# RWKV, attention and expert trunk on one core: `w_out` products leave the last RWKV steps, output norms go to VectorE with the bonus made ahead, two experts' matrices issued together

## The chip, the core and the metric

One core of a Trainium2 chip runs the kernel. A core has a matmul engine (TensorE, PE in the rows), VectorE (DVE), ScalarE (ACT), GpSimd (POOL) and SyncE (SP, which here only issues transfers), each with an instruction stream of its own; they meet through semaphores. Sixteen DMA engines carry the transfers that SP, ACT and POOL issue. The metric is the device time of one execution in microseconds, as the median of several runs.

## What is computed

Two layers of a trunk over 512 latent tokens and 256 context tokens, 1024 channels, float32. In each layer three mixers read slices of one input projection: a two-directional RWKV recurrence (256 channels, four heads), an S5 recurrence (256) and windowed attention (512). Their outputs side by side go through `w_out`, a residual and a norm; then each token goes through two of 32 experts.

```python
def trunk_layer(x, xc, ...):                # last layer: no context output
    proj = (x * (1.0 + sc1) + sh1) @ w_in   # and the same of xc
    yr, yr_c = rwkv_mixer(...); ys, ys_c = s5_mixer(...); ya, ya_c = attention_mixer(...)
    mix = jnp.concatenate([yr, ys, ya], axis=-1) @ w_out
    x = layer_norm(DEEPNORM_ALPHA * x + gt1 * mix, ln1_g, ln1_b)
    h = x * (1.0 + sc2) + sh2
    y = hier_moe(h, *moe_params)            # top 2 of 8 experts in the best of 4 groups
    x = layer_norm(DEEPNORM_ALPHA * x + gt2 * y, ln2_g, ln2_b)

def rwkv_output(y, feats, g2, r_k, gn_w, gn_b):
    mu = jnp.mean(y, axis=-1, keepdims=True)
    var = jnp.mean(jnp.square(y - mu), axis=-1, keepdims=True)
    yn = ((y - mu) * lax.rsqrt(var + GN_EPS)).reshape(B, L, RWKV_WIDTH) * gn_w + gn_b
    bonus = jnp.sum(r * k_sum * r_k, axis=-1, keepdims=True) * v
    gate = jax.nn.sigmoid(g_lo) @ g2
    return (yn + bonus) * gate
```

## The kernel before

Tokens go in tiles of 128: layer 0 has six (0 and 1 are context, 2 to 5 latent), layer 1 only the four latent ones. A layer runs through these stages:

- **Input side**: the projection and S5.
- **RWKV** (`rwkv`): `front` and `back` build each tile's features; `inverse` and `solves` prepare chunks; then twelve `steps`, n = 0 to 11, carry the state through the chunks in both directions at once. The directions use banks of the matmul's accumulators named f and g. Within a step L631 multiplies by the state, L633 adds on DVE, L640 forms the new state, L647 and L653 put it away on DVE; L672 and L676 are the step's output, and L682 adds it to the tile's `y`. When all steps are through, `finish` takes tiles 3 and 4, then 2 and 5: mean, variance (the squares `sq` are made on POOL, L699), the reciprocal root on POOL (L702, L703), a multiply on DVE (L706), `gn_w`, `gn_b` on POOL (L707, L708), the bonus `v` times `bon` on DVE (L710), added on POOL (L711), the gate from a matmul (L713) multiplied on DVE (L714). The result is turned on PE (L59) and copied by ACT to `yo`. The context tiles finish after step 3.
- **Mixing** (`mixing`), a generator that other work draws from. `part(i)` multiplies the S5 and attention rows of tile i by `w_out`: twelve products of 128x512 on PE (L1602), then DVE gates them and adds the residual (L1609, L1610, two of each), and ACT stores the sum to memory. `norm(i)` loads it back as `q` (L1635, ACT), adds the RWKV rows' four products (L1644) to it (L1650), takes moments (L1651, L1652), makes `h` (L1655, L1656) and its transposes; `logits` is the router's matmul (L1394, L1397, L1400). `affine` makes the residual of the next norm from `q` (L1668, L1669). `choose` picks groups and experts for two tiles with some fifty small DVE instructions and scatters tokens to a table (L1472, POOL); `Route.finish` reads the table back (L1502, L1504, L1506, L1509) and makes the index lists.
- **Experts**: POOL gathers tokens (L1869) and 32 experts run in turn. `Weights.get(e)` issues three matrices of 2 MB each on SP; three experts have buffers.

What sets the order: the program order is the priority, and a scheduler then orders each engine's stream by it and by the data. The table `FILL` says, for each point of `rwkv`, how many units of attention, of the modulation and of `mixing` are drawn in there. After steps 6, 8 and 9 it drew the six parts, after 10 and 11 the norms of tiles 0 and 1 and their choice. `k.rest` and `k.normed` tell the caller how far the generator is to be run behind `rwkv` and behind the first expert's weights. `q` and two small tiles of the norms had three buffers.

Of the kernel before, what the change touches and what calls it, by code (L numbers as in the profile page):

```python
# [1545 lines left out]
def mixing(k, l, sO, sR, before, yd, ys, x_src, x1, hd, NTOK):  # L1546
# [132 lines left out]
    late = {}  # L1679
    if t0 == 0:  # L1680
        for j in range(2):
            hT, late[j] = norm(j)
# [4 lines left out]
        rank = rt.choose([0, 1])
        k.rest = True
        yield
    for j, i in enumerate((3, 4)):  # L1690
        hT, late[i] = norm(i)
        if j == 0 and t0 == 0:
            rank()
        rt.logits(j, hT)
        yield
    late[3]()
    hT, late[2] = norm(2)
    rank = rt.choose([3 - t0, 4 - t0])
    rt.logits(0, hT)
    late[4]()  # L1700
    hT, late[5] = norm(5)
    rt.logits(1, hT)
# [581 lines left out]
```

## Time and profile before

| | us |
|---|---|
| median of three runs (2838.5 to 2843.27) | 2841.53 |
| the profiled execution, its own time | 2848.87 |
| its span in the trace | 2847.1 |
| layer 0: last steps, finish, norms, router (740 to 910) | 170 |
| layer 1: the same (2160 to 2277) | 117 |
| layer 0: the first expert's matmul starts at | 910.08 |
| layer 1: the same | 2276.55 |

The span is the profiled execution without what lies around it; times in the rows count from its start. A row of a timeline gives the start, the length, the engine, the line, the operation with its output and inputs and, in brackets, how long the engine stood idle before it and what ended that. PE rows put several instructions together (x32), and one product of the kernel appears there as two records. In the stage table each engine has its busy time and, in brackets, its instructions; PEclk is TensorE's granted clock as a share of its upper level.

### The profile page before, as it was taken

The numbers are of one execution on the slowest core, as the hardware profiler recorded it, in microseconds if no ns is written. First come the engines' busy times: TensorE is split into PE (matmuls) and PEld (weight loads), VectorE is DVE, ScalarE is ACT, GpSimd is POOL, SyncE is SP. The second block draws the span as 40 slices with busy tenths as digits, with TensorE's granted clock in tenths as the row PEclk, the third lists the DMA queues.
The fourth block names the chain that finished last, engine by engine and source line by source line (L and its number), as shares of the span: only waits on it lengthen the run. The fifth ranks groups of instructions, "written<-read, shape, count | busy, mean of one in ns | idle before, by whom it ended". The sixth has DMA issues, their size and how long they took to land. (4 is left out here: it accounts for less than half of the span.)

```text
span 2847.1 us, 43425 instructions
## 1 busy us (share of the span) xinstructions
PE 2222.6 (78%) x16189; PEld 1485.8 (52%) x16189; DVE 1165.4 (41%) x2836; ACT 517.5 (18%) x1264; POOL 805.1 (28%) x1160
## 2 busy tenths in 40 slices
PE   5898677888973978999856788787797397888882
PEld 3787455666542544555525676565554254454441
DVE  7972556563384000101026873656545611111113
ACT  3222333222010000101015122333120100000001
POOL 2651534330152111101016653434334210111002
PEclk8999788598986999999987898688798698999996
DMA  8334567665547899989974325556774799989994
GB/s 243 95 95 118 152 189 200 173 183 172 191 172 239 347 416 368 392 336 375 380 280 117 82 57 148 134 143 162 217 226 155 229 378 417 419 348 367 376 421 185
DMA packets 413931, 690.01 MB, mean 242 GB/s; under 512 B 148882, under 2 KB 318610, under 8 KB 397232
## 3 DMA queue, kind: packets, MB, share of 16 engines
q1 hardware_dynamic: 310368, 594.85, 58.7%
q10 hardware_dynamic: 74960, 56.54, 6.8%
q0 software_dynamic: 28288, 34.32, 3.7%
q8 instruction: 210, 3.44, 0.5%
q14 instruction: 105, 0.86, 0.1%
HBM read 606.46 MB, written 95.47 MB: 247 GB/s over the span
## 5 line engine op out<-in xcount | busy, mean ns | idle before, releaser
L1776 PE MATMUL b_m<-w,xT 128*64 128x256 f32 x4928 | 596.2, 398 | 128.4 <-DMA w<-in_expert_w_gate_dram 80.4
L1776 PEld LDWEIGHTS b_m<-w,xT 128*64 128x64 f32 x4928 | 391.8, 143 | 335.2 <-issue 148.1
L243 PE MATMUL b_m<-xT,win 128*128 128x256 f32 (+1 forms) x1416 | 275.9, 355 | 8.5 <-POOL xT L167 3.7
L243 PEld LDWEIGHTS b_m<-xT,win 128*128 128x128 f32 x1416 | 232.6, 201 | 42.6 <-POOL xT L167 4.5
L1800 PE MATMUL b_m<-w,aT 128*64 128x512 f32 x1024 | 230.9, 592 | 1.1 <-issue 0.6
L1789 DVE COPY aT<-b_m 128x256 f32<-128x256 f32 x64 | 27.2, 425 | 475.2 <-PE b_m L59 475.2
L1806 POOL DMA_INDIRECT yb<-y,dx x64 | 63.9, 998 | 427.7 <-DVEq L1921 257.1
L1800 PEld LDWEIGHTS b_m<-w,aT 128*64 128x64 f32 x1024 | 75.5, 137 | 118.0 <-issue 108.8
L876 PE MATMUL b_a<-kz,qb 128*128 128x128 f32 (+2 forms) x416 | 116.4, 424 | 17.1 <-ACT pr L897 12.7
L1778 ACT ACTIVATE act<-b_m 128x256 f32<-128x256 f32 x64 | 24.5, 383 | 577.6 <-PE b_m L1776 565.9
L1779 DVE TENSOR_TENSOR act<-act,b_m 128x256 f32<-128x256 f32 x64 | 27.0, 421 | 233.6 <-PE b_m L1776 233.6
L1602 PE MATMUL b_a<-wo,yt 128*128 128x512 f32 x240 | 112.7, 614 | 0.0
L876 PEld LDWEIGHTS b_a<-kz,qb 128*128 128x128 f32 x416 | 79.0, 237 | 43.5 <-ACT pr L897 15.4
L127 PE MATMUL b_a<-wmod,cc 128*32 128x128 f32 x1280 | 69.0, 325 | 33.6 <-DMA wmod<-in_w_mod_dram 29.7
L1806 POOL DMA_INDIRECT yb<-yo,dx x13 | 12.9, 995 | 289.6 <-ACTq L1921 146.7
L59 PE MATMUL b_a<-idf,pr 128*128 128x128 f32 x320 | 59.4, 311 | 27.5 <-ACT pr L897 9.9
L656 POOL TENSOR_TENSOR sn<-st,gc 128x128 f32<-128x128 f32 x44 | 25.1, 570 | 182.2 <-DVE st L647 168.4
L1869 POOL DMA_INDIRECT xg<-hd,ix x32 | 33.0, 1030 | 152.8 <-PE b_m L59 122.7
L1602 PEld LDWEIGHTS b_a<-wo,yt 128*128 128x128 f32 x240 | 44.0, 193 | 47.4 <-issue 46.0
L127 PEld LDWEIGHTS b_a<-wmod,cc 128*32 128x32 f32 x1280 | 40.5, 125 | 53.6 <-DMA wmod<-in_w_mod_dram 20.4
L551 POOL TENSOR_TENSOR tl<-Bm,Xh 112x4 f32<-112x4 f32 (+13 forms) x112 | 38.6, 344 | 90.6 <-DVE Xh L552 43.5
L503 PE MATMUL b_g<-ar,bz 128*128 128x128 f32 (+1 forms) x384 | 61.0, 322 | 3.8 <-ACT bz L495 3.8
(536 smaller groups left out, 3965.0 us busy)
## 6 DMA issues: line engine op xcount, KB each, us to landing
w<-in_expert_w_gate_dram SPq DMA_DIRECT2D x64, 2048.0 KB
w<-in_expert_w_up_dram SPq DMA_DIRECT2D x64, 2048.0 KB
w<-in_expert_w_down_dram SPq DMA_DIRECT2D x64, 2048.0 KB
wmod<-in_w_mod_dram SPq DMA_DIRECT2D x80, 512.0 KB
rec<-rec SPq DMA_DIRECT2D x40, 512.0 KB
win<-in_w_in_dram SPq DMA_DIRECT2D x16, 1024.0 KB
wmod<-in_w_mod_dram SPq DMA_DIRECT2D x4, 2048.0 KB
sca<-sc SPq DMA_DIRECT2D x24, 256.0 KB
```

What stands on the lines that cost most here:

```text
L59: k.nc.tensor.transpose(out, x, k.idf[r:r + n, r:r + n])
L127: nc.tensor.matmul(p[32 * g:32 * g + 32, :], k.cc[:, kk, :], wt[:, kk, :], start=kk < 4, stop=kk >= 4, tile_position=(0, 32 * g))
L243: nc.tensor.matmul(p[:, :n], wt[u][:, kk, j * 128:j * 128 + 128], xT[v][:, kk, c0:c0 + n], start=kk == 0 and q == 0, stop=kk == 7 and q == 2)
L503: nc.tensor.matmul(pv[:, cp, q, 0:n, :], bk[:, hp, q, cp].rearrange("p s t -> p (s t)"), ar[:, 0:n, cp, q, :], start=True, stop=True)
L551: eng.tensor_tensor(t[:, 0:n, j:32], Bm[:, r0:r1, j:j + 1].to_broadcast([112, n, w]), x.to_broadcast([112, n, w]), op=ALU.mult)
L876: nc.tensor.matmul(dst, qb[:, 2 * v + e, :], kz[:, v, r, 128 * keys[c][0]:128 * keys[f - 1][0] + 128], start=c == 0 or (c == 4 and r == 0) ...
L1602: nc.tensor.matmul(ps[h], y[:, kt, :], wo[:, kt, 512 * h:512 * h + 512], start=kt == 0, stop=kt == 5)
L1776: mm = nc.tensor.matmul(p[64 * h:64 * h + 64, 0:256], xT[:, kk, :], w[:, kk, 256 * h:256 * h + 256], start=kk == 0, stop=kk == 7)
L1789: k.nc.vector.tensor_copy(aT, pa[:, 0:256].rearrange("p (j x) -> p j x", j=2))
L1800: nc.tensor.matmul(py[64 * s:64 * s + 64, :], aT[:, j, 64 * h:64 * h + 64], wd[:, q, 512 * s:512 * s + 512], start=q == 0, stop=q == 3)
L1806: sc = nc.gpsimd.indirect_dma_start(out=yb, out_offset=bass.IndirectOffsetOnAxis(ap=dst, axis=0), in_=y, in_offset=None, bounds_check=3071 ...
L1869: return nc.gpsimd.indirect_dma_start(out=out, out_offset=None, in_=hd, in_offset=bass.IndirectOffsetOnAxis(ap=idx, axis=0), bounds_check= ...
```

## The change

- **Parts.** `FILL` draws nothing of `mixing` any more from step 8 on (and, in layer 0, takes the place of its last four entries with an empty one). In layer 0 parts 3, 4, 2 and 5 now come after `rwkv`, with norms 0 and 1 between them: 3, 4, norm 0, 2, norm 1, 5. In layer 1 parts 2 and 5 come there.
- **Finish.** The bonus is made ahead: `VT` is multiplied by `bon` on DVE and `gn_b` added on POOL, for tiles 0 and 1 after step 3 and for the others after step 8 in program order. In `finish` the squares, the `gn_w` multiply and the bonus' addition are on DVE; POOL keeps only L702 and L703.
- **Norms and choice.** The choice for tiles 3 and 4 comes behind the norm of tile 5, with the affines. `q` and the small tiles have four buffers; all stores of `h` are ACT's.
- **Matrices.** The second expert's matrices are issued right behind the first's.

```diff
+    def bonus(tiles):
+
+        for i in tiles:
+            V.tensor_tensor(h4(VT[i]), h4(VT[i]), bon[i][:, :, None].to_broadcast([128, 4, 64]), op=ALU.mult)
+            G.tensor_tensor(VT[i], VT[i], pb['gn_b'], op=ALU.add)
...
     def finish(tiles):
...
-            G.tensor_tensor(s2, y, y, op=ALU.mult)
+            V.tensor_tensor(s2, y, y, op=ALU.mult)
...
-            G.tensor_tensor(y, y, pb['gn_w'], op=ALU.mult)
-            G.tensor_tensor(y, y, pb['gn_b'], op=ALU.add)
-            s2 = Rp.tile([128, 256], F32, name='sq', bufs=1)
-            V.tensor_tensor(h4(s2), h4(VT[i]), bon[i][:, :, None].to_broadcast([128, 4, 64]), op=ALU.mult)
-            G.tensor_tensor(y, y, s2, op=ALU.add)
+            V.tensor_tensor(y, y, pb['gn_w'], op=ALU.mult)
+            V.tensor_tensor(y, y, VT[i], op=ALU.add)
...
         if n == 3 and emit_ctx:
+            bonus((0, 1))
             finish((0, 1))
...
+        if n == 8:
+            bonus((3, 4, 2, 5))
     outputs(11)
...
-        t2 = self.P.tile([16, 2, NB * 64, 2], I32, name='f_t2', tag='q', bufs=3)
+        t2 = self.P.tile([16, 2, NB * 64, 2], I32, name='f_t2', tag='q', bufs=4)
...
-        t = R.tile([128, D], F32, name='q', bufs=3)
+        t = R.tile([128, D], F32, name='q', bufs=4)
...
-        k.store = (nc.sync if i in (2, 5) else A).dma_start(hd[r], h)
+        A.dma_start(hd[r], h)
...
-    while parts:
-        part(parts.pop(0))
-        if not parts:
-            gated(0, P)
-            k.rest = t0 > 0
+    gated(0, P)
+    late = {}
+
+    def normed(j, i):
+        hT, late[i] = norm(i)
+        rt.logits(j, hT)
+
+    for x in (parts.pop(0), parts.pop(0), (0, 0), parts.pop(0), (1, 1), parts.pop(0)) if t0 == 0 else parts:
+        if isinstance(x, tuple):
+            normed(*x)
+        else:
+            part(x)
         yield
...
     if t0 == 0:
-        for j in range(2):
-            hT, late[j] = norm(j)
-            rt.logits(j, hT)
-            yield
+        rank = rt.choose([0, 1])
+    k.rest = True
+    yield
+    normed(0, 3)
+    yield
+    if t0 == 0:
+        rank()
         late[0]()
+    normed(1, 4)
+    yield
+    normed(0, 2)
+    if t0 == 0:
         late[1]()
...
+    normed(1, 5)
     k.normed = True
     yield
+    rank = rt.choose([3 - t0, 4 - t0], rt.pair)
+    late[3]()
     rank()
+    late[4]()
     rt.choose([2 - t0, 5 - t0])()
...
                 wts.get(0)
+                wts.get(1)
...
-                with tc.issue_after(k.store.ins):
-                    wts.get(1)
```

The built programs show where the instructions stand. Behind the change the lines of the source have moved: L1602 is L1611, L1644 is L1653, L713 is L718, L714 is L719, L699 is L707, L700 is L708, L1609 and L1610 are L1618 and L1619.

PE in layer 0, from the end of step 8 to step 10 (`b_a` with `yt` is a product with `w_out`, the L631 of banks f and g begin a step), before:

```order
L640 MATMUL b_g<-rec_7112 64x64 x4
L672 MATMUL b_g<-sb_6743,rec_6943 64x128 x2
L676 MATMUL b_g<-rec_6943 64x64 x4
L1602 MATMUL b_a<-wo_6766,yt 128x512 x16
L631 MATMUL b_f<-sb_7133,rec_7244 64x128 x2
L631 MATMUL b_g<-sb_7137,rec_7249 64x128 x2
L1602 MATMUL b_a<-wo_6766,yt 128x512 x2
L640 MATMUL b_f<-rec_7244 64x64 x4
L672 MATMUL b_f<-sb_6964,rec_7107 64x128
L640 MATMUL b_g<-rec_7249 64x64 x4
L672 MATMUL b_f<-sb_6964,rec_7107 64x128
```

and now:

```order
L1611 MATMUL b_a<-wo_6764,yt 128x512
L640 MATMUL b_g<-rec_7110 64x64 x4
L672 MATMUL b_g<-sb_6741,rec_6941 64x128 x2
L676 MATMUL b_g<-rec_6941 64x64 x4
L1611 MATMUL b_a<-wo_6764,yt 128x512
L631 MATMUL b_f<-sb_7131,rec_7163 64x128 x2
L1611 MATMUL b_a<-wo_6764,yt 128x512
L631 MATMUL b_g<-sb_7135,rec_7168 64x128 x2
L640 MATMUL b_f<-rec_7163 64x64 x4
L672 MATMUL b_f<-sb_6962,rec_7105 64x128 x2
L640 MATMUL b_g<-rec_7168 64x64 x4
L676 MATMUL b_f<-rec_7105 64x64 x4
```

The run of 16 ahead of L631 and the pair behind it are gone (the run of 22 stood at the end of the same step); one product stands after each output of step 8 and one between the two L631.

PE in layer 0 behind the last step (`g` with `gl` is the gate of `finish`, L59 turns `y`, `yo` is an output's product in a norm), before:

```order
L672 MATMUL b_g<-sb_7377,rec_7503 64x128 x2
L676 MATMUL b_g<-rec_7503 64x64 x4
L713 MATMUL b_f<-g_2613,gl_3726 128x256
L59 MATMUL b_a<-idf,h 128x128 x8
L1394 MATMUL b_a<-hT,wr 64x128 x8
L1644 MATMUL b_a<-wo_7157,yo 128x512
L1397 MATMUL b_a<-sel_108,r_lt 128x36
L1644 MATMUL b_a<-wo_7157,yo 128x512 x3
L59 MATMUL b_f<-idf,y 128x128 x2
```

and now:

```order
L676 MATMUL b_g<-rec_7268 64x64 x4
L718 MATMUL b_f<-g_2613,gl_3726 128x256
L1611 MATMUL b_a<-wo_6764,yt 128x512 x6
L59 MATMUL b_f<-idf,y 128x128 x2
L718 MATMUL b_f<-g_2613,gl_4058 128x256
L1611 MATMUL b_a<-wo_6764,yt 128x512 x2
L59 MATMUL b_f<-idf,y 128x128 x2
L718 MATMUL b_f<-g_2613,gl_3063 128x256
L1611 MATMUL b_a<-wo_6764,yt 128x512 x4
L59 MATMUL b_f<-idf,y 128x128 x2
L718 MATMUL b_f<-g_2613,gl_3395 128x256
L1611 MATMUL b_a<-wo_6764,yt 128x512
```

Behind the steps PE had the first context tile's router and the norms; now it has the products of the last parts between the turns of `finish`.

DVE in layer 1, `finish` of tiles 3 and 4 from the squares on (`sq` are the squares, `vt` with `b` the bonus, `b_f` the gate), before:

```order
L700 TENSOR_REDUCE gvv<-sq 128x4
L697 TENSOR_TENSOR y<-y,gmv 128x256
L706 TENSOR_TENSOR y<-y,gvv 128x256
L710 TENSOR_TENSOR sq<-vt_19102,b_3_19140 128x256
L706 TENSOR_TENSOR y<-y,gvv 128x256
L1860 MEMSET xg_22344 128x1024
L714 TENSOR_TENSOR y<-y,b_f 128x256
L710 TENSOR_TENSOR sq<-vt_19427,b_4_19465 128x256
L1860 MEMSET xo_22346 128x1024
L700 TENSOR_REDUCE gvv<-sq 128x4
L714 TENSOR_TENSOR y<-y,b_f 128x256
```

and now:

```order
L708 TENSOR_REDUCE gvv<-sq 128x4
L707 TENSOR_TENSOR sq<-y 128x256
L708 TENSOR_REDUCE gvv<-sq 128x4
L707 TENSOR_TENSOR sq<-y 128x256
L714 TENSOR_TENSOR y<-y,gvv 128x256 x2
L715 TENSOR_TENSOR y<-y,b_gn_w 128x256 x2
L716 TENSOR_TENSOR y<-y,vt_19096 128x256
L716 TENSOR_TENSOR y<-y,vt_19421 128x256
L719 TENSOR_TENSOR y<-y,b_f 128x256
L708 TENSOR_REDUCE gvv<-sq 128x4
L1618 TENSOR_TENSOR oq<-b_a,gt 128x512
L719 TENSOR_TENSOR y<-y,b_f 128x256
```

The bonus (L710) is gone from here; the squares (L707), the `gn_w` multiply (L715) and the addition of the bonus (L716) stand on DVE in a row with the others.

## Rows read from the trace of the kernel before

**Rows 1.** Stage table, layer 0: busy us per engine, granted clock, DMA share:
```profile
core 0: us, PE busy (x) PEld busy (x) DVE busy (x) ACT busy (x) POOL busy (x), PEclk, DMA share, GB/s
...
740.00:797.00 57.00, 57.00 (x313) 31.04 (x312) 27.21 (x50) 1.29 (x4) 6.00 (x8) 1.00 0.52 171
...
797.00:835.00 38.00, 20.62 (x86) 11.55 (x86) 30.53 (x68) 4.10 (x10) 23.10 (x29) 0.78 0.35 118
...
835.00:874.00 39.00, 21.23 (x109) 12.92 (x108) 29.74 (x67) 4.68 (x12) 14.76 (x15) 0.72 0.69 249
```

**Rows 2.** PE timeline, layer 0 (start, length, engine, line, [wait]):
```profile
747.03 14.00 PE L1602 MATMUL b_a<-wo,yt 128*128 128x512 f32 x32
...
766.15 19.15 PE L1602 MATMUL b_a<-wo,yt 128*128 128x512 f32 x44
...
796.75 0.38 PE L713 MATMUL b_f<-g,gl 128*128 128x256 f32 x1
```

**Rows 3.** DVE timeline, layer 0, steps 10 and 11:
```profile
785.93 0.43 DVE L633 TENSOR_TENSOR rec<-b_f,rec 64x256 f32<-64x256 f32 x1
...
793.72 0.43 DVE L633 TENSOR_TENSOR rec<-b_f,rec 64x256 f32<-64x256 f32 x1
```

**Rows 4.** DVE timeline, layer 0, the finish:
```profile
802.30 0.42 DVE L682 TENSOR_TENSOR y<-b_g,y 64x256 f32<-64x256 f32 x1
...
808.14 0.43 DVE L706 TENSOR_TENSOR y<-y,gvv 128x256 f32<-128x256 f32 x1 [1.47 <-POOL gvv L703]
...
831.28 0.42 DVE L714 TENSOR_TENSOR y<-y,b_f 128x256 f32<-128x256 f32 x1 [1.34 <-POOL y L711]
```

**Rows 5.** POOL timeline, layer 0, the finish:
```profile
815.06 1.59 POOL L708 TENSOR_TENSOR y<-y,b_gn_b 128x256 f32<-128x256 f32 x1
```

**Rows 6.** DVE timeline, the last norm of layer 0 and of layer 1:
```profile
863.08 0.69 DVE L1650 TENSOR_TENSOR q<-b_g,q 128x512 f32<-128x512 f32 x1 [7.06 <-DMA q<-mixq]
...
872.06 1.28 DVE L1656 SCALAR_TENSOR_TENSOR h<-h,r_sb,hb 128x1024 f32<-128x1024 f32 x1 [0.39 <-POOL r_sb L87]
...
2224.45 0.69 DVE L1650 TENSOR_TENSOR q<-b_g,q 128x512 f32<-128x512 f32 x1 [5.31 <-DMA q<-mixq]
...
2236.66 1.28 DVE L1656 SCALAR_TENSOR_TENSOR h<-h,r_sb,hb 128x1024 f32<-128x1024 f32 x1 [0.38 <-POOL r_sb L87]
```

**Rows 7.** PE timeline, the first expert of each layer:
```profile
910.08 5.17 PE L1776 MATMUL b_m<-w,xT 128*64 128x256 f32 x28
...
2276.55 5.68 PE L1776 MATMUL b_m<-w,xT 128*64 128x256 f32 x38
```

**Rows 8.** PE timeline, layer 1, before step 10 and behind step 11:
```profile
2159.97 7.99 PE L1602 MATMUL b_a<-wo,yt 128*128 128x512 f32 x18
...
2176.46 0.70 PE L713 MATMUL b_f<-g,gl 128*128 128x256 f32 x2
```

**Rows 9.** PE timeline, layer 0, norms:
```profile
829.91 2.05 PE L1644 MATMUL b_g<-wo,yo 128*128 128x512 f32 x2 [5.88 <-DVE q L1650]
...
836.27 2.74 PE L1644 MATMUL b_g<-wo,yo 128*128 128x512 f32 x6
```

**Rows 10.** Stage table, slices around those two rows (columns as in rows 1):
```profile
824.00:830.00 6.00, 0.12 (x2) 0.12 (x1) 4.07 (x13) 0.21 (x1) 4.47 (x6) 0.89 0.29 87
...
830.00:836.00 6.00, 6.00 (x10) 2.70 (x11) 4.72 (x18) 0.37 (x1) 3.27 (x6) 0.54 0.34 87
...
836.00:844.00 8.00, 7.36 (x44) 4.31 (x42) 8.00 (x22) 1.81 (x5) 1.89 (x3) 1.00 1.02 412
```

**Rows 11.** SP queue, layer 0, between the two experts' matrices:
```profile
833.11 0.33 SPq L1838 DMA_DIRECT2D w<-in_expert_w_gate_dram  x1
...
855.98 17.72 SPq L1658 DMA_DIRECT2D hd<-h  x2
...
873.80 0.37 SPq L1838 DMA_DIRECT2D w<-in_expert_w_gate_dram  x1
```

**Rows 12.** DVE timeline, layer 1, end of the steps:
```profile
2176.57 0.42 DVE L682 TENSOR_TENSOR y<-b_g,y 64x256 f32<-64x256 f32 x1 [0.30 <-PE b_g L676]
```

More of the change, by code (lines that the diff above doesn't have):

```diff
@@ L685, in output, with h4 @@
             seen.add((i, cp))
+    def bonus(tiles):
+        for i in tiles:
+            V.tensor_tensor(h4(VT[i]), h4(VT[i]), bon[i][:, :, None].to_broadcast([128, 4, 64]), op=ALU.mult)
+            G.tensor_tensor(VT[i], VT[i], pb['gn_b'], op=ALU.add)
+    def h4(z):
+        return z.rearrange("p (h n) -> p h n", h=4)
     def finish(tiles):
@@ L691, in finish @@
         vv = Rp.tile([128, n, 4], F32, name='gvv', bufs=2)
-        h4 = lambda z: z.rearrange("p (h n) -> p h n", h=4)
         for j, i in enumerate(tiles):
@@ L1398, in logits, with choose @@
         if j == 0:
-            self.L = self.new('lg', [128, 2, 36])
+            self.pair, self.L = getattr(self, 'L', None), self.new('lg', [128, 2, 36])
         nc.vector.tensor_tensor(self.L[:, j], p[:, 128:164], self.br, op=ALU.add)
-    def choose(self, ts):
-        k, nc, new, L = self.k, self.k.nc, self.new, self.L
+    def choose(self, ts, L=None):
+        k, nc, new = self.k, self.k.nc, self.new
+        L = self.L if L is None else L
         V = nc.vector
@@ L1645, in norm @@
         st = rt.new('st', [128, 2, 6])
-        mv = rt.new('mv', [128, 2], bufs=3)
-        sb = rt.new('sb', [128, 1], bufs=3)
+        mv = rt.new('mv', [128, 2], bufs=4)
+        sb = rt.new('sb', [128, 1], bufs=4)
         for h in range(2):
@@ L1671, in norm @@
         return hT, affine
-    while parts:
-        part(parts.pop(0))
-        if not parts:
-            gated(0, P)
-            k.rest = t0 > 0
+    gated(0, P)
[8 more added lines that the diff above has]
+            part(x)
         yield
-    late = {}
     if t0 == 0:
-        for j in range(2):
-            hT, late[j] = norm(j)
-            rt.logits(j, hT)
-            yield
+        rank = rt.choose([0, 1])
[5 more added lines that the diff above has]
+        rank()
         late[0]()
+    normed(1, 4)
+    yield
+    normed(0, 2)
+    if t0 == 0:
         late[1]()
[L1687 to L1702, printed above, removed]
+    yield
+    normed(1, 5)
     k.normed = True
     yield
+    rank = rt.choose([3 - t0, 4 - t0], rt.pair)
+    late[3]()
     rank()
+    late[4]()
     rt.choose([2 - t0, 5 - t0])()
@@ L2037, in combine @@
             put(None, None, None, None)
-FILL = ({'front': ((1, 0, 0), (1, 3, 0)), 'back': ((1, 3, 0),), 'inverse': ((4, 6, 0), (4, 4, 0)), 'step': ((3, 2, 0), (3, 3, 0), (2, 4, 0), (3, 3, 0), (3, 3, 0), (0, 2, 2), (0, 2, 0), (0, 0, 2), (0, 0, 2), (0, 0, 2), (0, 0, 1))}, {'front': ((1, 0, 0), (1, 0, 0)), 'back': ((0, 0, 0), (1, 4, 0), (1, 2, 0), (1, 2, 0)), 'inverse': ((1, 9, 0),), 'step': ((2, 5, 0), (1, 4, 0), (2, 6, 0), (2, 3, 0), (1, 1, 0), (0, 0, 2), (1, 0, 0), (0, 0, 1), (0, 0, 1), (0, 0, 0))})
+FILL = ({'front': ((1, 0, 0), (1, 3, 0)), 'back': ((1, 3, 0),), 'inverse': ((4, 6, 0), (4, 4, 0)), 'step': ((3, 2, 0), (3, 3, 0), (2, 4, 0), (3, 3, 0), (3, 3, 0), (0, 2, 2), (0, 2, 0), (0, 0, 0))}, {'front': ((1, 0, 0), (1, 0, 0)), 'back': ((0, 0, 0), (1, 4, 0), (1, 2, 0), (1, 2, 0)), 'inverse': ((1, 9, 0),), 'step': ((2, 5, 0), (1, 4, 0), (2, 6, 0), (2, 3, 0), (1, 1, 0), (0, 0, 2), (1, 0, 0), (0, 0, 0))})
 TILES = ({'z': (0,), 't': (0, 0, 0, 0, 0, 1, 0, 1), 'e': (1, 1, 1, 2, 1, 2, 2, 1), 'r': (0, 1, 0, 1, 0, 1, 0, 2), 'o': (0, 0)}, {'z': (1,), 't': (0, 0, 0, 0, 0, 0, 0, 0), 'e': (1, 1, 1, 1, 2, 1, 1, 1), 'r': (0, 1, 0, 1, 0, 1, 0, 1), 'o': (0, 0)})
```

## The prediction

> **What bounds the kernel now.** I read the stage table first, then the engines' timelines inside it, then SyncE's queue. In each layer only one stretch is touched: the last RWKV steps and what follows them, up to the experts' first matmul. Behind that the experts run from their weights, and I take them to move as a block with their start.
>
> *The steps of layer 0.* From 740 to 797 us PE is busy in 57.00 of 57 us at a granted clock of 1.00, DVE in 27 [rows 1]: PE is the limit. Its timeline says with what: 16 products with `w_out` (L1602) stand in one run of 14.00 us and 22 in one of 19.15, each ahead of the L631 with which the next step begins [rows 2]. (A product shows as two records, so a run of 32 records is 16 products; 19.15 / 22 = 0.87 us each.) Step 11, with four L1644 but no product ahead of it, comes 7.8 us behind step 10 (793.72 - 785.93) [rows 3]. The steps end where PE reaches L713, at 796.75 [rows 2]; I call this T.
>
> *From T to the last norm.* Here PE is half idle (20.62 of 38 us, 21.23 of 39) and DVE leads with 30.53 and 29.74 [rows 1]. In the output's norm DVE waits for POOL: 1.47 us for the reciprocal root ahead of L706, 1.34 for the sum of L711 ahead of L714 [rows 4]; a single POOL instruction there takes up to 1.59 us [rows 5]. Then comes a wait of 7.06 us for tile 5's `q` [rows 6], which has three buffers. The stage's last row is L1656 at 872.06, done 873.34 [rows 6]. Scatters, table and gather then take 36.7 us to the first expert at 910.08 [rows 7].
>
> *Layer 1* is the same without the context tiles: nine products in one run of 7.99 us ahead of step 10, T at 2176.46 [rows 8], 5.31 us of waiting for `q`, the last L1656 at 2236.66 [rows 6], the first expert at 2276.55 [rows 7].
>
> **The change, part by part.** The profiled execution took 2848.87 us, 7.3 (0.26%) above the median 2841.53 of the runs shown. All differences below are read in it and taken off the median.
>
> *Layer 0, the steps.* Of the 72 products, 31 stood before step 8's second direction and 41 between it and T. Now 24 stand ahead of it, 7 lie singly between the steps and 41 behind T. So 41 leave: 41 x 0.87 = 35.7 us. Four L1644 go with them, at 2.74 / 3 = 0.91 [rows 9] 3.6. Sum 39.3; some of those that leave stood alone and cost more than in a run, so I take 40 as what PE saves. What is late next is the step itself, a chain of PE, DVE and PE that three times is no longer covered; 2 us for that. **Gain 38**, T = 758.8 (bounds 30, if the steps keep the 7.8 us of step 11, and 41).
>
> *Layer 0, from T to the last L1656.* I count DVE's instructions between the last L682 and the last L1656 in both built orders: 512-wide 20 before and 40 after, 1024-wide 19 and 23, 256-wide 23 and 28, small ones 57 and 42 (the choice for tiles 3 and 4 goes behind). At 0.69, 1.28 and 0.42 [rows 4, 6] and an estimated 0.16 us for a small one that is 13.8 + 5.1 + 2.1 - 2.4 = 18.6; instructions in a row overlap a little, so 17 us more work. Before, 70.6 us lie between that L682's end (802.30 + 0.42 [rows 4]) and 873.34, by the same count 54 of work and 16.5 idle. After, the work is 71. Its idle time: POOL's root, once for each pair of tiles, 3.5; the first norm stands behind 17 products and four L1644 on PE, some 21 us with the finish's own matmuls, for which DVE has 17, so 4; the next norm's L1644 stand behind a run of eleven products (11 x 0.87 = 9.6 us) for which DVE has next to nothing, 10; tile 5's store and load of `q`, now with a fourth buffer, all but 2 under other work; the roots of the norms, 2. Together 21.5. So the last L1656 ends 1 + 71 + 21.5 = 93.5 behind T, at 852.3 against 873.34: of the 38 us **21 stay**. The second run of eleven (tile 5) costs nothing by this count, since 20 us of affines and norms are queued on DVE then; without that cover it is 9.6 more.
>
> *The clock.* The products' place in the steps had a granted clock of 1.00; behind T it is 0.78 and 0.72 [rows 1]. An L1644, the same size, took 2.05 us behind a wait of 5.88 us, at 0.54, and 0.91 in a run in the next slice, at 1.00 [rows 9, 10]. So the first one or two products behind a wait may cost 1.1 more; **2 us back** (bounds 0 and 28 x 1.1 = 31).
>
> *The tail of layer 0.* The choice for tiles 3 and 4 now starts behind the last norm; its scatters run straight into those of 2 and 5 and end, by my count of small DVE instructions, 2 us later behind L1656. L1533 and both L1509 stand ahead of L1506 on DVE, 1.5. **3.5 back** (bounds 0 and 6).
>
> *Bonus ahead, stores, matrices.* Six DVE and six POOL instructions of 256 columns land in the front stage, at 0.42 [rows 4] and about 1 us; DVE has other work there and POOL is not the limit: **1 back**. The order of front, back and inverse shifts with them, which I can only bound: 6 us either way. Two `h` stores go from SP to ACT. SP spent 17.72 us in them, with the second expert's matrices behind [rows 11]. Those are now issued with the first's, some ahead of `xq` and `yt` of the last parts. The time gains nothing by it: PE has expert 0 to do first.
>
> Layer 0: 21 - 2 - 3.5 - 1 = **14.5**.
>
> *Layer 1.* Five of the nine products of the run go behind T, where the finish leaves PE free; the other four lie in earlier gaps: 5 x 0.87 = 4.4. From the last L682 (2177.0 [rows 12]) to the end of the last L1656 (2237.94) there are 61 us, by the count 41 of DVE work; after, it is 42 (four 512-wide and four 256-wide more, two 1024-wide less, five small ones less), and of 20 us idle some 8 are left: POOL's sums are gone, its roots stay (twice 1.8, and 2 in the norms), `q` has four buffers for four tiles. So 11, and 4.4 before it; the tail gives 3 back: **12.5** (bounds 7 and 18).
>
> Sum: 14.5 + 12.5 = 27; 2841.5 - 27 = **2814.5 us**.
>
> **The rivals.**
> - *Handed back.* The products behind T are serial with the norms, layer 0 ends where it did, and layer 1's 12.5 are left: 2829. For it: DVE is the limit behind T and gets 17 us more. Against: the 93.5 us must become 108.
> - *More.* T at 756, behind it only the 16.5 us idle of before, no longer tail: layer 0 gains 28.8, layer 1 its 18: 2795.
> - *Weights in the way.* Both experts' matrices, six of 2 MB, move while tile 5's `q` is stored and loaded. At the 412 GB/s of a full slice [rows 10] that is 31 us if all of it stood before that load: 2845, no change. For it: SP's two stores took 17.72 us [rows 11]. Against: by the order the load comes some 60 us behind the first of them.
> - *The clock stays low behind T* (slower). Place: the 39 products behind T (17, 11 and 11) that DVE then waits for. At 2.05 instead of 0.91 us [rows 9, 10] they cost 39 x 1.14 = 44: 2859. It decides at 27 / 39 = 0.7 us more per product, from about 1.6 us each. Against: the runs are 10 us long, and the run in rows 10's last slice was at the upper level again.
>   The Trainium skill (TensorE: Matmul & The Clock Gate, section "Part 1: The HAM clock gate") has the throttled state, 1.2 GHz, as the default that only activity lifts to 2.4; that speaks against taking work out of a full PE and putting it behind waits. The trace agrees in the doubling, 0.91 to 2.05; by the rule at its worst the time is this rival's, by the rows' mean it is the forecast's.
> - *Not what it says.* Seven products stay in the steps; if steps 8 to 11 kept their length in another wait, nothing would be won in layer 0 and the tails would be longer: 2841.
>
> **How the numbers follow.** 0.2% is 5.7 us, about what a measurement of this kernel can tell from no change. Forecast (2804 to 2824) 0.55; handed back 0.17; more 0.12; weights 0.07; low clock 0.06; not what it says 0.03. Faster 0.55 + 0.17 + 0.12 = 0.84; within 0.07 + 0.03 = 0.10; slower 0.06. The range takes in "handed back" with the front stage's 6 us, and most of "more": 2797 to 2836; some 0.2 is left out.
>
> **What would show it.** On PE at most single L1602 between the last four steps, and L713 near 759, give or take the front stage's 6. On DVE nothing idle on a POOL sum in the finish; one idle stretch of some 10 us in layer 0 ahead of an L1650, put down to PE's L1644; none over 3 us for `q`. The last L1656 ends some 94 us behind L713 in layer 0, some 51 in layer 1. The first experts start near 895 and 2249. Products at 0.87 us in their runs; from 1.6 on the clock rival holds. If the last L1656 ends over 105 us behind T in layer 0, the idle time that I gave DVE was wrong; if T is late, the length of an uncovered step.

## The result and the profile after

The changed kernel took 2808.35 us (median of four runs, 2802.48 to 2811.68) against 2842.40 (2838.5 to 2846.85; four runs, where the table ahead has three) for the kernel before: a ratio of 0.9883, 95% interval 0.986 to 0.9905, 34 us faster where 27 were forecast. The profiled execution took 2802.48 us (span 2800.6), 46.4 less than the one before. Each profile is one execution; about 13 of the 46 lie in layer 1's front stage, which also differs between executions of one kernel (below).

From here line numbers are those of the changed kernel: the product with `w_out` is L1611 (was L1602), its reader L1618 (L1609), the norm's product L1653 (L1644), its reader L1659 (L1650), the last affine L1665 (L1656), the gate L718 (L713), the root of the finish L711 (L703). These landmarks cut the profiled executions into pieces, each measured from the one before it (us; "first step" is the first L633 of the layer, "last y" the end of its last L682, "last h" the end of its last L1665, "first expert" its first L1787; the 67 to 68 us between the experts of layer 0 and layer 1's front, alike in all columns, are left out):

| piece | before | after | w1_late | swap_mid | prod_back | prod_back_swap | swap_rank |
|---|---|---|---|---|---|---|---|
| layer 0, first step to last y | 235.4 | 185.1 | 186.3 | 185.1 | 217.4 | 220.5 | 178.2 |
| to last h | 70.6 | 106.8 | 105.0 | 93.3 | 78.9 | 70.4 | 88.6 |
| to first expert | 36.7 | 31.5 | 35.1 | 33.7 | 33.9 | 36.1 | 40.1 |
| sum of the three | 342.7 | 323.4 | 326.4 | 312.1 | 330.2 | 327.0 | 306.9 |
| experts of layer 0 | 555.9 | 555.6 | 552.9 | 557.2 | 556.1 | 555.3 | 553.8 |
| layer 1, front to first step | 493.7 | 480.6 | 482.2 | 488.3 | 489.0 | 483.3 | 483.2 |
| to last y | 150.5 | 147.5 | 148.5 | 143.1 | 149.7 | 152.5 | 146.7 |
| to last h | 60.9 | 50.4 | 54.3 | 49.8 | 46.2 | 46.0 | 49.8 |
| to first expert | 38.6 | 36.3 | 43.7 | 37.6 | 36.1 | 37.5 | 37.6 |

Stage table of the changed kernel, layer 0, behind the last steps (columns as in rows 1; the first stretch is the 57 us up to L718, the second and third the products and norms, the fourth tile 5's store):

```profile
697.40:754.40 57.00, 54.66 (x424) 33.28 (x421) 25.21 (x53) 3.58 (x13) 7.83 (x7) 0.91 0.66 212
754.40:797.00 42.60, 39.45 (x123) 18.89 (x122) 25.16 (x52) 2.83 (x7) 6.37 (x7) 1.00 0.59 215
797.00:833.00 36.00, 27.72 (x105) 13.37 (x103) 33.82 (x59) 2.89 (x7) 7.74 (x11) 0.98 0.68 261
833.00:846.00 13.00, 0.00 (x0) 0.00 (x0) 2.74 (x7) 0.20 (x1) 1.53 (x3) 0.50 1.01 404
846.00:862.00 16.00, 6.72 (x56) 5.41 (x57) 8.94 (x22) 2.88 (x6) 7.06 (x8) 0.70 0.19 72
```

PE's timeline, where rows 2 had runs of 16 and 22 products inside the steps:

```profile
744.43 0.62 PE L631 MATMUL b_g<-sb,rec 128*64 128x128 f32 x4 [2.35 <-DVE sb L653]
...
754.43 0.70 PE L718 MATMUL b_f<-g,gl 128*128 128x256 f32 x2
...
788.19 9.69 PE L1611 MATMUL b_a<-wo,yt 128*128 128x512 f32 x22
...
814.01 9.69 PE L1611 MATMUL b_a<-wo,yt 128*128 128x512 f32 x22
```

T is 754.43, the steps now wait for each other (2.35 us, where a run of products stood), and the two runs of eleven take 9.69 us, 0.88 a product, at a granted clock of 1.00 and 0.98. DVE's timeline behind T, the rows in which it waited:

```profile
759.23 0.76 DVE L714 TENSOR_TENSOR y<-y,gvv 128x256 f32<-128x256 f32 x2 [1.82 <-POOL gvv L711]
...
774.01 0.69 DVE L1618 TENSOR_TENSOR oq<-b_a,gt 128x512 f32<-128x512 f32 x1 [3.23 <-PE b_a L1611]
...
789.90 0.69 DVE L1659 TENSOR_TENSOR q<-b_g,q 128x512 f32<-128x512 f32 x1 [4.64 <-DMA q<-mixq]
...
797.06 0.69 DVE L1618 TENSOR_TENSOR oq<-b_a,gt 128x512 f32<-128x512 f32 x1 [5.17 <-PE b_a L1611]
...
844.96 0.91 DVE L1871 MEMSET xg<- 128x1024 f32 x1 [10.06 <-DMA mixq<-xq]
...
849.93 0.69 DVE L1659 TENSOR_TENSOR q<-b_g,q 128x512 f32<-128x512 f32 x1 [2.79 <-DMA q<-mixq]
...
860.50 1.28 DVE L1665 SCALAR_TENSOR_TENSOR h<-h,r_sb,hb 128x1024 f32<-128x1024 f32 x1 [3.83 <-POOL r_sb L87]
```

The finish waits for no POOL sum any more (rows 4's 1.34 is gone), only for the root, 1.82 and once more 1.44. The last L1665 ends at 861.78, 107 us behind T. The waits of 10.06 and 2.79 have one cause. In the first DVE stands ahead of a MEMSET whose memory tile 5's store (`mixq<-xq`) still reads, in the second it waits for the load that follows this store. ACT's queue shows tile 3's store and load of `q`, then tile 5's; SP's queue shows the matrices (L1849) of the second expert (770 to 785) and of the first (824 to 828; `w1_mid` below shows which is which), then the table's read (L1511):

```profile
769.96 0.33 ACTq L1620 DMA_DIRECT2D mixq<-xq  x1
772.90 0.34 ACTq L1644 DMA_DIRECT2D q<-mixq  x1
...
829.49 0.33 ACTq L1620 DMA_DIRECT2D mixq<-xq  x1
844.75 0.33 ACTq L1644 DMA_DIRECT2D q<-mixq  x1
```

```profile
770.46 0.33 SPq L1849 DMA_DIRECT2D w<-in_expert_w_gate_dram  x1
...
785.38 0.45 SPq L1849 DMA_DIRECT2D w<-in_expert_w_down_dram  x1
823.76 0.33 SPq L1849 DMA_DIRECT2D w<-in_expert_w_gate_dram  x1
...
827.60 0.38 SPq L1849 DMA_DIRECT2D w<-in_expert_w_down_dram  x1
881.27 0.34 SPq L1511 DMA_DIRECT2D r_ti<-tab  x1
```

Each of the two loads goes when the store has landed, so tile 3's store took 2.9 us and tile 5's 15.3: three matrices had been issued 2 to 6 us ahead of the latter, and in 833 to 846 the DMA engines are full (1.01, 404 GB/s) while PE does nothing. The Trainium skill (DMA: Bandwidth & Descriptors, section "Issuing engines are not separate DMA queues") says that transfers started by any engine run on the same 16 DMA engines and interleave; the trace agrees, a store on ACT's queue being held by loads on SP's.

The last wait, 3.83 us for `r_sb`, is on POOL: four scatters of the router's choice stand between the two instructions that make the root.

```profile
853.60 0.22 POOL L86 TENSOR_SCALAR r_sb<-r_mv 128x1 f32<-128x1 f32 x1 [5.88 <-DVE r_pos L1475]
854.42 1.59 POOL L1481 DMA_INDIRECT tab<-tokd,r_pos  x1 [0.60 <-issue]
...
858.89 0.97 POOL L1481 DMA_INDIRECT tab<-tokd,r_pos  x1 [0.30 <-issue]
859.88 0.59 POOL L87 TENSOR_TENSOR r_sb<-r_sb,mh 128x1 f32<-128x1 f32 x1
...
878.78 0.95 POOL L1481 DMA_INDIRECT tab<-tokd,r_pos  x1 [0.31 <-issue]
```

The last scatter ends at 879.73 and the table is read 1.5 us later, at 881.27; the first expert starts at 893.28 and, in layer 1, at 2230.59 (rows 7: 910.08 and 2276.55).

### The profile page after: what moved, and what is told of

It reads as the page before. It is cut to its first block, busy times and chain, and to the rows that moved or that the text cites. A ratio compares the mean times of both kernels' runs of the same rounds, so it can differ in the third digit from the quotient of the medians.

```text
span 2800.6 us, 43418 instructions
## 1 busy us (share of the span) xinstructions
PE 2177.6 (78%) x16189; PEld 1456.8 (52%) x16189; DVE 1175.7 (42%) x2866; ACT 518.5 (19%) x1264; POOL 775.8 (28%) x1130
## 5 line engine op out<-in xcount | busy, mean ns | idle before, releaser
L1787 PE MATMUL b_m<-w,xT 128*64 128x256 f32 x4928 | 595.0, 397 | 129.4 <-DMA w<-in_expert_w_gate_dram 78.7
L1787 PEld LDWEIGHTS b_m<-w,xT 128*64 128x64 f32 x4928 | 391.7, 143 | 335.3 <-issue 151.3
L1611 PE MATMUL b_a<-wo,yt 128*128 128x512 f32 x240 | 114.9, 616 | 0.0
L884 PEld LDWEIGHTS b_a<-kz,qb 128*128 128x128 f32 x416 | 76.6, 234 | 33.7 <-issue 12.1
L59 PE MATMUL b_a<-idf,pr 128*128 128x128 f32 x320 | 59.0, 308 | 24.9 <-DVE pt L928 10.8
L1611 PEld LDWEIGHTS b_a<-wo,yt 128*128 128x128 f32 x240 | 43.6, 193 | 43.5 <-issue 42.1
L127 PEld LDWEIGHTS b_a<-wmod,cc 128*32 128x32 f32 x1280 | 37.8, 121 | 52.2 <-DMA wmod<-in_w_mod_dram 31.5
L1816 DVE TENSOR_TENSOR y<-b_m,gate 128x512 f32<-128x512 f32 x32 | 22.1, 692 | 95.0 <-PE b_m L1811 95.0
L551 POOL TENSOR_TENSOR tl<-Bm,Xh 112x4 f32<-112x4 f32 (+13 forms) x112 | 37.5, 335 | 83.0 <-DVE Xh L552 48.7
```

What stands on the lines that cost most here:

```text
L59: k.nc.tensor.transpose(out, x, k.idf[r:r + n, r:r + n])
L127: nc.tensor.matmul(p[32 * g:32 * g + 32, :], k.cc[:, kk, :], wt[:, kk, :], start=kk < 4, stop=kk >= 4, tile_position=(0, 32 * g))
L551: eng.tensor_tensor(t[:, 0:n, j:32], Bm[:, r0:r1, j:j + 1].to_broadcast([112, n, w]), x.to_broadcast([112, n, w]), op=ALU.mult)
L884: nc.tensor.matmul(dst, qb[:, 2 * v + e, :], kz[:, v, r, 128 * keys[c][0]:128 * keys[f - 1][0] + 128], start=c == 0 or (c == 4 and r == 0) ...
L1611: nc.tensor.matmul(ps[h], y[:, kt, :], wo[:, kt, 512 * h:512 * h + 512], start=kt == 0, stop=kt == 5)
L1787: mm = nc.tensor.matmul(p[64 * h:64 * h + 64, 0:256], xT[:, kk, :], w[:, kk, 256 * h:256 * h + 256], start=kk == 0, stop=kk == 7)
```

## The experiments

Theory A after the first look: the gain is the steps' 42 us and the finish's waits; what eats it is tile 5's `q` behind the second expert's matrices. Rivals: the matrices' place does not matter; the products are hidden in either place; the gain is that of the bonus made ahead, by way of the front stages. All runs are on chips that ran the kernel before beside them; ratios are to it.

**The second expert's matrices later.** `w1_mid` holds them until tile 5's `q` has been read, `w1_late` until the last affine, about where they were before:

```
-                wts.get(1)
...
+                wts.hold = k.store
+                wts.get(1)
+                wts.hold = None
```

with `k.store` the instruction waited for (the reader L1659, or L1665) and a dependency on it in `fetch`.

> The changed kernel, but the second expert's three matrices wait for the first L1659 of tile 5's norm, that is until its q has been loaded. Theory A (the matrices and tile 5's store and load of q share the DMA engines): that store, 15.3 us in the changed kernel, takes about 3 again, the last L1665 of layer 0 ends about 95 us behind T instead of 107, the matrices are through before the scatters end, the tail stays at 31 to 35 us; total about 2798 to 2802. Rival B (the matrices' place does not matter, DVE or POOL sets the end): within 3 us of the changed kernel's 2808.

> The changed kernel, but the second expert's matrices wait for the last L1665 (h of tile 5), about where the kernel before issued them. Theory A: the last L1665 comes about 12 us nearer to T, and the wait from the last scatter to the read of the table grows from 1.5 us back to about 9, so layer 0 gains 3 and layer 1 loses some: 2804 to 2810. Rival B: 2808 with neither of the two moved.

`w1_mid`: 2813.48 us, 0.9888 (0.9848 to 0.9928), no gain. ACT's queue and SP's queue of `w1_mid`:

```profile
831.43 0.33 ACTq L1620 DMA_DIRECT2D mixq<-xq  x1
846.65 0.33 ACTq L1644 DMA_DIRECT2D q<-mixq  x1
```

```profile
825.75 0.33 SPq L1849 DMA_DIRECT2D w<-in_expert_w_gate_dram  x1
...
854.11 0.33 SPq L1849 DMA_DIRECT2D w<-in_expert_w_gate_dram  x1
```

The store still takes 15.2 us: the three ahead of it are the first expert's, whose memory comes free late, so the expectation named the wrong expert. `w1_late`: 2823.88, 0.9934 (0.9906 to 0.9962): some 14 us slower than the change, where 2804 to 2810 was expected. The last h is no nearer (105.0), and both tails are longer (35.1 and 43.7 us). Layer 0's second set of matrices, issued at 865 to 868, moves under the scatters, and the table (L1511) is read 6.2 us behind the last scatter's end (882.35 + 1.27), where the changed kernel has 1.5. POOL's last scatter and SP's read in `w1_late`:

```profile
882.35 1.27 POOL L1481 DMA_INDIRECT tab<-tokd,r_pos  x1 [0.30 <-issue]
```

```profile
889.86 0.34 SPq L1511 DMA_DIRECT2D r_ti<-tab  x1
```

Layer 1 has more of it: there the read comes 9.8 us behind the last scatter's end (2236.02 against 2226.21), 3.6 in the changed kernel. So issuing both experts' matrices early is worth something, most of it by the tails.

**The finish as before.** `fin_old` has the squares, the `gn_w` multiply and both additions on POOL again and the bonus made inside.

> The changed kernel with the finish of the kernel before (bonus in it, squares, gn_w, gn_b and the sum on POOL). Theory A: layer 1's stretch from the last L682 to the last norm is 10 us longer again, layer 0's 2 to 5, nothing else moves: 2820. Rival C (the bonus, put by the scheduler into the front stages, is what shortened layer 1's front by 12.7 us): that front is long again too, 2833. If the front's length is chance of one execution, it differs from run to run whatever the finish is.

2828.90, 0.9932 (0.9906 to 0.9958), 14 us slower than the change, where 12 were expected. DVE's timeline of `fin_old`, second finish (old line numbers):

```profile
779.02 0.42 DVE L700 TENSOR_REDUCE gvv<-sq 128x4 f32<-128x256 f32 x1 [2.12 <-POOL sq L699]
...
786.41 0.42 DVE L714 TENSOR_TENSOR y<-y,b_f 128x256 f32<-128x256 f32 x1 [2.78 <-POOL y L711]
```

These waits are back; the scheduler also placed the products otherwise (37 instead of 31 ahead of T), so 14 is the price of the finish with what hangs on it. The profiled execution is the slowest of nine (2846.28) and does not place the 14: from the last y to the last h it has 109.1 us in layer 0 and 52.3 in layer 1, each 2 above the changed kernel, where 10 had been expected for layer 1.

**The products back in the steps.** `prod_back` draws the last four parts' products after steps 8 and 9 as before (two parts after each in layer 0's table, one in layer 1's), and

```
-    for x in (parts.pop(0), parts.pop(0), (0, 0), parts.pop(0), (1, 1), parts.pop(0)) if t0 == 0 else parts:
+    for x in (parts.pop(0), parts.pop(0), parts.pop(0), parts.pop(0), (0, 0), (1, 1)) if t0 == 0 else parts:
```

> The changed kernel with the products of the last four parts drawn after steps 8 and 9 again (in layer 0 all four ahead of the context norms). Theory A: T of layer 0 is 36 to 40 us later and the stretch behind it 15 to 25 shorter, T of layer 1 4 later: 2822 to 2832. Rival D (the gain comes from the finish and the choice, the products are hidden either way): within 4 us of 2808.

2813.68, 0.9886 (0.9851 to 0.992), the same as the change within the intervals, where 2822 to 2832 was expected. PE's timeline of `prod_back` has the runs inside the steps again:

```profile
739.41 17.76 PE L1611 MATMUL b_a<-wo,yt 128*128 128x512 f32 x41
...
762.28 19.15 PE L1611 MATMUL b_a<-wo,yt 128*128 128x512 f32 x44
...
791.48 0.70 PE L718 MATMUL b_f<-g,gl 128*128 128x256 f32 x2
```

T is 37 us later and the last h stands 28 us nearer behind it. As the change stands, the headline edit brings nothing that the runs can tell. The 34 are the rest of the change: by the runs around this one the finish (14), the matrices (14) and the `q` buffer (8). The later choice and the stores of `h` on ACT were not tried alone.

**The changed kernel again, and the collision removed.** `swap_mid` gives the memory that comes free early to the first expert, whose matrices then go at 768 to 783, and holds the second's as `w1_mid` does:

```
-                wts = Weights(k, l, Wb, Wa)
+                wts = Weights(k, l, Wa, Wb)
```

> The changed kernel itself, unaltered, for a comparison on the chip of the runs beside it and for a second profile. If layer 1's front stage (480.6 us in its first profile, 493.7 in the kernel before) is chance of an execution, it comes out anywhere from 480 to 490 here; if the bonus made ahead shortens it, it stays 480 to 483. Total 2808 +- 6 where the kernel before gives 2842.

> The changed kernel with the two first experts' buffers exchanged (the first expert gets the memory that comes free early, the second that which comes free at about 824 us) and the second expert's matrices held until tile 5's q has been loaded. What w1_mid left: tile 5's store of q (15 us) ran against the first expert's own matrices, issued at 824 to 830. Theory E (that collision is what makes the last norm late): the store takes 3 us, the last L1665 ends 93 to 96 us behind the last L682 instead of 105 to 107, the tail stays 31 to 35: 10 to 14 us below after_again. Rival F (POOL's scatters or DVE's queue set the last norm): it stays within 4 us of after_again.

`after_again`: 2811.00, 0.9872 (0.9843 to 0.9902). From the end of the experts to the first L631 of layer 1 its profile has 551.0 us, the first profile of the same kernel 546.4, the kernel before 559.5. `swap_mid`: 2796.87, 0.9832 (0.9809 to 0.9855), 14 us below it on the same chip, though the two intervals overlap at their ends. ACT's queue, SP's queue and DVE's last affine in `swap_mid`:

```profile
826.60 0.33 ACTq L1620 DMA_DIRECT2D mixq<-xq  x1
830.01 0.33 ACTq L1644 DMA_DIRECT2D q<-mixq  x1
```

```profile
783.29 0.45 SPq L1849 DMA_DIRECT2D w<-in_expert_w_down_dram  x1
836.61 0.33 SPq L1849 DMA_DIRECT2D w<-in_expert_w_gate_dram  x1
```

```profile
844.82 1.29 DVE L1665 SCALAR_TENSOR_TENSOR h<-h,r_sb,hb 128x1024 f32<-128x1024 f32 x1 [4.05 <-POOL r_sb L87]
```

The store takes 3.4 us instead of 15.3, tile 5's wait is gone, and the last h is 93.3 behind the last y. `w1_mid` differs by the exchanged memory alone.

**Three buffers for `q`.** `q3` sets `bufs=3` in the two places of the change.

> The changed kernel with three buffers for q, as before. By the prediction the fourth buffer hides 5 us of waiting in each layer: 7 to 10 us above after_again, with waits for q of 5 us and more in both layers. Rival G (the load waits for the store of the same tile, not for a buffer): layer 0 unchanged, layer 1 5 us longer.

2819.29, 0.9904 (0.9885 to 0.9924), 8 us above `after_again` by the medians; the intervals overlap. DVE's timeline of `q3`, tile 4's norm in layer 0 and the last norm of layer 1:

```profile
812.74 0.69 DVE L1659 TENSOR_TENSOR q<-b_g,q 128x512 f32<-128x512 f32 x1 [13.61 <-DMA q<-mixq]
...
2211.87 1.29 DVE L1659 TENSOR_TENSOR q<-b_g,q 128x512 f32<-128x512 f32 x2 [5.86 <-DMA q<-mixq]
```

In layer 0 the 13.61 largely takes the place of other waits: the three pieces sum to 325.2 against 323.4. The fourth buffer shows in layer 1, where the last h comes 64.3 us behind the last y instead of 50.4.

**The bonus inside the finish, all on DVE.** `fin_dve` drops `bonus` and makes it in `finish` with one multiply and one more addition on DVE for each tile.

> The changed kernel with the bonus back inside the finish, but all of the finish on DVE (bonus product, gn_b and both sums), POOL keeping only the root. Theory H (the finish is faster because POOL is out of it; where the bonus is made matters little): the finish is longer by 8 instructions of 0.42 us, 3 us in each layer, total 5 to 7 us above after_again. Rival C (the bonus ahead changes the order of the front stages, and that is where 10 us or more come from): layer 1's front is 491 to 494 us and layer 0's last L682 comes 10 us later, total 20 us above.

2806.51, 0.985 (0.9823 to 0.9877): not slower, with 39 products ahead of T. That the bonus is made ahead brings nothing that the runs can tell; that POOL is out of the finish does. Layer 1's front took 482.4 us here, without a bonus ahead, and 480.6 to 491.6 in all runs but the kernel before's 493.7. The 491.6 is `fin_old`'s, so the two longest fronts are those of the two kernels with the finish on POOL; one of them is a slow execution, and chance is not excluded.

**With the collision gone.** On `swap_mid`: the products back in the steps (`prod_back_swap`), the first choice's `rank()` moved in the code from between the norms of tiles 3 and 4 to behind tile 5's (`swap_rank`), the finish of `fin_dve` (`swap_findve`).

> The version with the first expert's matrices sent first and the second's held until tile 5's q is loaded, but with the w_out products of the last four parts drawn in the steps again, as before the change. Theory: putting those products behind the steps is worth 10 to 15 us once tile 5's store and load of q no longer stand under the matrices (layer 0: T earlier by 37, last h later behind it by some 25; in the changed kernel as it is the collision of 10 to 13 us ate that): 10 to 15 us slower than swap_mid, ratio to the kernel before 0.987 to 0.989. Rival: the products are hidden either way, in the steps or behind them, and their place is worth nothing: within 4 us of swap_mid.

> The same version, with the scatters of the first two context tiles' choice behind the last norm, so that POOL has none of them between the last norm's variance and its reciprocal root. Theory: DVE's last wait of 4 us for r_sb goes, all twelve scatters then stand in a row in the tail, on POOL, under the small DVE work of the later choices for all but 0 to 2 us: 2 to 4 us faster than swap_mid in layer 0. Rival: the tail is bound by POOL's scatters and grows by the time of the four that come later (4 to 5 us): no gain, or up to 2 us slower.

> The same version, with the whole finish on VectorE and the bonus made inside it again, not ahead. Theory (the place of the bonus does not matter, as the earlier run without the new order of matrices had it): within 4 us of swap_mid. Rival: made inside, it is four to six 256-column DVE instructions and as many additions more at 0.42 us behind the steps in each layer, where DVE is the limit: 4 to 8 us slower.

`prod_back_swap`: 2817.27, 0.9901 (0.9865 to 0.9938), on the same chip 17 us above `swap_rank` and 15 above `swap_findve`; sum of layer 0's pieces 327.0 against `swap_mid`'s 312.1. Now the products' place is worth some 15 us. `swap_findve`: 2802.67, 0.9862 (0.983 to 0.9893); its interval and `swap_mid`'s overlap, as expected.

`swap_rank`: 2799.80, 0.9848 (0.9815 to 0.9882), no gain. DVE's timeline of `swap_rank`:

```profile
839.84 1.28 DVE L1665 SCALAR_TENSOR_TENSOR h<-h,r_sb,hb 128x1024 f32<-128x1024 f32 x1 [0.69 <-POOL r_sb L87]
...
862.18 0.17 DVE L1475 CAST r_pos<-r_pf 128x4 int32<-128x4 f32 x1 [8.38 <-DMA tab<-tokd,r_pos]
```

The wait for `r_sb` fell from 4.05 to 0.69 and the last h came 4.7 us nearer, but the last choice's positions now waited 8.38 us for the first choice's scatters, whose buffer they reuse (two buffers, three choices), and the tail grew by 6.4. `rank_pos3` adds a buffer:

```
-new('pos', [128, 2, 2], I32)
+new('pos', [128, 2, 2], I32, 3)
```

> swap_rank with a third buffer for the integer positions from which a scatter reads its rows. In swap_rank the last choice's cast of the positions waited 8.38 us for the first choice's scatters, which now stand so late. Theory: that wait goes, the last four scatters follow straight behind the eight others (8 x 1.26 us), 4 to 5 us earlier, the table is read 4 to 5 us earlier and the first expert of layer 0 starts 40 to 41 us behind the end of the last step-to-norm stretch less that: 35 to 36 behind the last h; total 3 to 5 us below swap_rank. Rival: the scatters' transfers land no earlier than before because they queue behind the matrices that move by then, and the wait only goes from the cast to the table's read: the first expert stays at 40 behind the last h, no change.

2801.44, 0.9827 (0.9797 to 0.9858): as its rival had it, no change from `swap_rank`. DVE's timeline, POOL's last scatter and SP's read of the table in `rank_pos3`:

```profile
878.39 0.60 DVE L1518 TENSOR_SCALAR r_tf<-r_ti 32x192 f32<-32x192 int32 x2 [12.27 <-DMA r_ti<-tab]
```

```profile
869.19 0.95 POOL L1481 DMA_INDIRECT tab<-tokd,r_pos  x1 [0.30 <-issue]
```

```profile
876.66 0.34 SPq L1511 DMA_DIRECT2D r_ti<-tab  x1
```

The twelve scatters stand in a row and the cast no longer waits, but the read comes 6.5 us behind the last scatter's end, in `swap_rank` 1.7; the first expert is 39.1 behind the last h (40.1 in `swap_rank`). Twice the wait moved, from POOL's order to a buffer and from there to the table's read. `swap_mid`, its two successors and `swap_findve` can't be told apart: `swap_mid` has the lowest median, `rank_pos3` the lowest ratio. All four lie clearly below the kernel before, and their medians (2796.87 to 2802.67) below the changed kernel's (2808.35 and 2811.00).

## Why the prediction was right, and where not

The sum was right (2814.5 against 2808.35, in the forecast's own range 2804 to 2824), though two terms were wrong by 14 us each, with opposite signs: from T to the last h in layer 0 (93.5 forecast, 107.4 measured) and the two tails (6.5 us back forecast, 7.5 gained). That they cancelled is luck.

*The steps: right.* T 754.43 against 758.8; by the profiles 42.3 us earlier, not 38 (1 us beyond the bound of 41). The uncovered chain costs little: the 2.35 us above are PE's only wait of that kind in the last steps, and 2 were forecast. Where the other 4 us came from was not traced.

*From T to the last h: the work right, the idle time wrong.* Forecast 93.5 with 71 of DVE work and 21.5 idle; measured 107, beyond the 105 that I had named as the sign of wrong idle time. DVE's busy time in the stage table is 25.16 + 33.82 + 2.74 + 8.94 = 70.7, so the work was counted well and the idle time is 36. By terms:

| idle on DVE | forecast | measured |
|---|---|---|
| POOL's root in the finish | 3.5 | 3.3 (1.82, 1.44) |
| first norm behind its products | 4 | 3.2 (ahead of a part's L1618) |
| run of eleven products | 10 | 5.2 (ahead of a part's L1618) |
| `q` of tiles 4 and 5 | 2 | 17.5 (4.64, 10.06, 2.79) |
| roots of the norms | 2 | 4.1 (3.83, 0.22) |

The rest of the 36 is waits of under 1 us. The step that failed is "tile 5's store and load of `q`, now with a fourth buffer, all but 2 under other work". The rival "weights in the way" had the mechanism and the wrong matrices: it counted back from the first of six, which turned out to be one of the second expert's, and set the rival aside because the load came 60 us later. Three of the six, the first expert's, went at 823.76 to 827.60, where tile 5's run of products (823.70) and the last L1653 (827.52) ended, 2 to 6 us ahead of tile 5's store. The trace of before had such a collision in it, behind the 7.06 us for `q` [rows 6]. There the load waited for a buffer, and the store that was to free it (`x<-q`, issued at 850.96) landed late, in full DMA engines (0.96 in 845 to 851, 1.01 in 851 to 855), behind the first expert's matrices of 833.11 [rows 11]. ACT's timeline in the kernel before:

```profile
858.92 0.21 ACT L1424 ACTIVATE r_ge<-r_gd 128x8 f32<-128x8 f32 x1 [8.25 <-DMA x<-q]
```

The rival's evidence was also misread: the 17.72 us of [rows 11] are not time that SP spent in two stores, but two issues in one row, at 855.98 and 873.37, the second right behind the last `h` of before (873.34). `swap_mid` takes the collision away, and its 93.3 from last y to last h meets the forecast.

*The tail and the matrices: wrong, the other way.* I gave the tail 3.5 back, and "The time gains nothing by it" to the matrices. The tail became 5.2 shorter in layer 0 and 2.3 in layer 1, and `w1_late` shows why: with the second expert's matrices moving under the scatters, the table is read 6.2 us behind the last scatter; before, a scatter took 9.9 us to land (the median of the two whose landing the trace has), now 3.0. DMA issues of before and of after, 840 to 885 us (line, count, median us from issue to landing):

```profile
tab<-tokd,r_pos POOLq DMA_INDIRECT x9, 9.9
```

```profile
tab<-tokd,r_pos POOLq DMA_INDIRECT x12, 3.0
```

In all, `w1_late` puts the early issue at some 14 us, about what the collision took (`swap_mid`).

*The clock: right that it would hold,* and the 2 us for it were not needed. The products behind T ran at 0.88 us with a granted clock of 1.00, and 0.98, so the rival of 2859 falls. PE had been busy in 39.45 of 42.6 and 27.72 of 36 us there, and the clock fell to 0.50, the lower level, where PE did nothing for 13 us, in the stretch of tile 5's store.

*The other rivals.* "Handed back" has two halves. Its number did not come: the last h stood 107 us behind T, one short of its 108, but T was 4 us earlier than forecast and the tail shorter, and layer 0's pieces fell by 19.3 us (342.7 to 323.4), more than the 14.5 forecast. Its mechanism nearly held for the change as written: `prod_back` can't tell the products' move from nothing. It fails as a rule, since `prod_back_swap` makes the move some 15 us once the matrices are out of the way. "Not what it says" falls: T moved.

*Layer 1:* 12.5 forecast. From its first step to the first expert 234.2 us against 250.0: 3.0 to the last y (forecast 4.4), 10.5 in the finish and norms (forecast 11), and 2.3 in the tail, where I had 3 back. I gave the idle time that goes there to POOL's sums and to the fourth `q` buffer together; by the profiles, one for each kernel, it is mostly the buffer's: the stretch is 64.3 us in `q3` and only 52.3 in `fin_old`, against 50.4. The front stage's 13.1 between the two profiles, more than the 6 us that I allowed, are at least in part the chance of an execution, as the 480.6 to 491.6 of the experiments say; whether a kernel with POOL in the finish is some us longer there by itself was not settled. Without the front, the pieces of both layers fell by 35 us, close to the 34 of the medians.

*Bonus ahead:* I took 1 us back and did not ask what it buys: nothing that shows, by `fin_dve` and `swap_findve`.

## What to carry to other kernels

Give each load in a prediction the time at which its memory comes free, not the place of its issue in the code: of two experts issued at once, the one needed first got the memory that came free last, and its 6 MB then stood in front of a 512 KB store on the critical path. An edit's worth depends on the others: the same move of products was worth nothing that could be measured with that collision and some 15 us without it, so test a headline edit alone before crediting it. When a wait is removed near the end of a stage, look for the next holder first (here POOL's order, then a buffer, then the table's read).

## What the runs showed of the hardware

A 512 KB store took 2.9 us (`after`, tile 3) and 3.4 us (`swap_mid`, tile 5) with no matrix ahead of it, and 15.3 us (`after`, tile 5) behind three matrices of 2 MB issued up to 6 us ahead of it, at 404 GB/s in all. Scatters of 128 rows landed in 3.0 us (median of twelve, `after`) on quiet DMA engines and in 8.6 and 11.2 us (`before`) while matrices moved. One gap stays open. In `rank_pos3` the stage table shows the DMA engines quiet well ahead of the table's read:

```profile
868.00:870.00 2.00, 0.00 (x0) 0.00 (x0) 0.00 (x0) 0.00 (x0) 1.70 (x2) 0.50 0.42 112
870.00:872.00 2.00, 0.00 (x0) 0.00 (x0) 0.00 (x0) 0.00 (x0) 0.15 (x1) 0.50 0.01 1
...
874.00:876.00 2.00, 0.00 (x0) 0.00 (x0) 0.00 (x0) 0.00 (x0) 0.00 (x0) 0.50 0.00 0
```

From 870.2 to 876 no engine computes and next to nothing moves, yet the read is issued only at 876.66. What holds it was not measured.
